# Two-layer encoder trunk on one core: a fifth opening block per feed-forward network, head stacks made in one step, and part of the mixer's weight splitting moved to GpSimd

## The chip, the cores and the metric

The kernel runs on one core of a Trainium2 chip. The metric is the device time of one execution in microseconds (us). The engines are named as the profile names them: PE is the matrix engine (PEld its weight loads), DVE the vector engine, ACT the scalar engine, POOL is GpSimd, and SP is the engine whose queue issues nearly all DMAs (copies between the chip's memory and the core's own).

## The reference

Two layers, each with three sub-layers on 512 tokens of width 1024. Every sub-layer stands between two RMS norms and is added to the running `x`.

```python
def reference(x, ...):
    for layer in range(2):
        h = swiglu(rms_norm(x, g[0]), ffn_w_in[layer, 0], ffn_w_out[layer, 0])
        x = x + 0.5 * rms_norm(h, g[1])
        h = token_mixer(rms_norm(x, g[2]), mix_w_in[layer], ...)
        x = x + rms_norm(h, g[3])
        h = swiglu(rms_norm(x, g[4]), ffn_w_in[layer, 1], ffn_w_out[layer, 1])
        x = x + 0.5 * rms_norm(h, g[5])

def swiglu(h, w_in, w_out):            # w_in 1024 x 5632, w_out 2816 x 1024
    g, u = jnp.split(h @ w_in, 2, axis=-1)
    return (jax.nn.silu(g) * u) @ w_out
```

The mixer projects `h` once (1024 to 3600 columns), feeds 8 attention heads (a mixture of three dilated windows) and 4 heads of a matrix memory (mLSTM, with gates from 16 of the columns), and sends both through one output projection. All values are float32.

## The kernel before

**Precision.** PE multiplies a reduced 32-bit type (`F32R`). Each factor is therefore split into a high part (ACT casts it) and a low part (DVE subtracts the high part from the original), and each product is three matmuls: high by high, high by low, low by high. For weights this is `split_w` (L114 the cast, L115 the subtraction) and `halves_of` (L97 and L99); for activations it is `put` (L209 and L210). The weight tiles `raw`, `hi` and `lo` are rings of three.

**Four token tiles.** The 512 tokens are four tiles of 128. After a sub-layer `post` adds its result to `x` tile by tile, and `pre` norms a tile for the next sub-layer, transposes it on PE (`tr`, L191) and puts high and low parts into `xh` and `xl`. Both get their inverse root from `rsqrt_sum`, whose power (`rs_yo`, `rs_yi`, L136) is computed by POOL. The last sub-layer's second half (tiles 2 and 3) overlaps the next one's start, which works on tiles 0 and 1.

**Feed-forward network (FFN).** `ffn_in` has 22 blocks `f` of 128 gate columns `g` and 128 up columns `u`, 512 KB of weights each. The first `ne` of them run plainly: `block(f, left)` for tiles 0 and 1, all `ne` in turn, then `block(f, right)` for tiles 2 and 3, all `ne` in turn, with 48 matmuls of 256 columns each; both weights are loaded anew for the second round. Then `xx.finish()` (a cast `xh`, L228, and a subtraction `xl`, L229, of a sum of activations `xf`) and the other blocks by `seven(f)`, a scheme with seven products for a pair of halves: 84 matmuls (L255 to L257) instead of the plain 96. A `seven` needs sums of its weights (`ws`, L319 to L322), split in turn into high and low (L297, L299). Its order on PE, DVE and ACT is written by hand; everything else is ordered by the framework's scheduler.

**A slot shared by weights and activations.** The `u` weight of a `seven` is loaded into the tile `wu`:

```python
raw = chunk("wu", 17 + 2 * (f % 2)) if gu and not whole_f else raw_tile()
```

The slots 17 and 19 also hold the two parts of `xf`. Slot 17 is last read in `finish()`, behind the last plain block, which also writes part of what `finish()` follows; slot 19 is last read when tile 3 is put, ahead of the right blocks. The weights of the block `ne + 1` go to the ring instead. All these loads go out through SP's one queue, in order (L272).

**Mixer.** Four groups of natural projections (`proj_nat`, matmuls `nat`, L500 to L502) on tiles 0 and 1, then transposed projections (`mixer_proj_T`), then the four groups on tiles 2 and 3, with the gates made between them (`gates` on DVE, transposes `gnat`, L727, on PE). The heads follow, while the attention's projections run between them. `stack_pair` makes, for each pair of attention heads, stacks of keys (`kst`) and queries (high `qsh`, low `qsl`) from two transposes on PE each; the scores `sc` (L870, L871) read them, `sm` is the softmax, `pt` its transpose.

Of the kernel before, what the change touches and what calls it, by code (L numbers as in the profile page):

```python
# [10 lines left out]
F32 = mybir.dt.float32  # L11
# [4 lines left out]
ALU = mybir.AluOpType  # L16
# [4 lines left out]
NT = S // P  # L21
# [20 lines left out]
def trunk_kernel(ctx, tc, x, norm_gain, ffn_w_in, ffn_w_out, mix_w_in, conv_w, conv_b,  # L42
# [48 lines left out]
    def raw_tile():  # L91
        return wp.tile([P, 1056], F32, tag="raw", name="raw", bufs=3)

    def halves_of(src, n, after=None):
        hi = wp.tile([P, 1056], F32R, tag="hi", name="hi", bufs=3)
        lo = wp.tile([P, 1056], F32R, tag="lo", name="lo", bufs=3)
        A.copy(hi[:, :n], src)  # L97
        with tc.issue_after(after) if after else nullcontext():
            V.tensor_tensor(lo[:, :n], src, hi[:, :n].bitcast(F32), ALU.subtract)  # L99
        return [[w[:, q: q + 512].rearrange("p (k c) -> p k c", k=4) for w in (hi, lo)] for q in range(0, n, 512)]  # L100

    def split_w(load, n, k4, pieces=1):
        raw = raw_tile()
        hi = wp.tile([P, 1056], F32R, tag="hi", name="hi", bufs=3)
        lo = wp.tile([P, 1056], F32R, tag="lo", name="lo", bufs=3)
        m = n * k4

        def view(w):
            return w[:, :m].rearrange("p (k c) -> p k c", k=k4)
        step = k4 // pieces  # L110
        for k in range(0, k4, step):
            r, h, l = [view(w)[:, k: k + step] for w in (raw, hi, lo)]
            load(r, k)
            A.copy(h, r)  # L114
            V.tensor_tensor(l, r, h.bitcast(F32), ALU.subtract)  # L115
        return view(hi), view(lo)

    def mm3(ps, lh, ll, rh, rl, start, stop):
# [50 lines left out]
            c = slice(n * 512, (n + 1) * 512)  # L169
            V.scalar_tensor_tensor(xs[:, t, c], y[:, c], r, xs[:, t, c], ALU.mult, ALU.add)  # L170

    first_nt = []

    def pre(t, xn, xx, ps_of):
        ss = small("pre_ss", 2)
        opening = len(first_nt) < 2
        if opening:
            V.tensor_tensor_reduce(out=xn[:, 512:1024], in0=xs[:, t, 512:1024], in1=xs[:, t, 512:1024], op0=ALU.mult,
                                   op1=ALU.add, scale=1.0, scalar=0.0, accum_out=ss[:, 1:2])
        for n in range(1 if opening else 2):  # L180
            A.activation(junk, xs[:, t, n * 512: n * 512 + 512], AF.Square, accum_out=ss[:, n: n + 1])
        r = rsqrt_sum((ss[:, 0:1], ss[:, 1:2]), D, EPS, "i")
        for hf in range(2):
            c = slice(hf * 512, hf * 512 + 512)
            V.scalar_tensor_tensor(xn[:, c], xs[:, t, c], r, gpre[:, c], ALU.mult, ALU.mult)
            if opening and hf:
                first_nt.append(last_ins(mybir.EngineType.DVE))
            ps = ps_of("tr")
            for k in range(4):
                kk = hf * 4 + k  # L190
                PE.transpose(ps[:, k * P: (k + 1) * P], xn[:, kk * P: (kk + 1) * P], ident)  # L191
            xx.put(t, hf, ps.rearrange("p (k c) -> p k c", k=4))
# [68 lines left out]
    def ffn_in(layer, j, xx, late=None):  # L261
# [17 lines left out]
                hts[f] = hts[f][:, 0:512]  # L279
            return hts[f]  # L280

        def block(f, c, pieces=1, after=None):
            h = h_of(f) if hts[f] is None else hts[f]
            banks = []
            for gu in range(2):
                lo_k, hi_k = halves_of(load(f, gu, pieces, True)[:, :1024], 1024, after)
                ps = psA("gu")[:, c]
                for q, w2 in enumerate((lo_k, hi_k)):
                    product(ps, w2, [x[:, 4 * q: 4 * q + 4, c] for x in (xx.h, xx.l)], q == 0)
                banks.append(ps)  # L290
            sil = t2("sil", f % 2)[:, c]
            A.activation(sil, banks[0], AF.Silu)
            V.tensor_tensor(h[:, c], banks[1], sil, ALU.mult)
# [87 lines left out]
            V.tensor_tensor(h[:, left], a, sil0, ALU.mult)  # L381
            V.tensor_tensor(h[:, right], u1, g1, ALU.mult)

        ne = 4
        for f in range(ne):
            block(f, left, 2 if late and f == 0 else 1, first_nt[-1] if late and f == 0 else None)
            if late and f < 2:
                late[f]()
        for f in range(ne):
# [92 lines left out]
            V.scalar_tensor_tensor(qk[b % 4][:, b // 4, :], th[:, :512], 1.0, y[:, :512], ALU.add, ALU.mult)  # L482
        return qk

    def proj_nat(layer, xx, col, n, evac, tiles=range(NT), ps_of=None, per=1):
        xh, xl = xx.h, xx.l
        w = mix_w_in[layer].rearrange("(k p) c -> p k c", p=P)
        parts = []
        for q in range(2):
            def load(dst, _, q=q):  # L490
                nc.sync.dma_start(dst, w[:, q * 4: q * 4 + 4, col: col + n])
            parts.append(split_w(load, n, 4))
        for t0 in tiles[::per]:
            ps = (ps_of or psA)("nat")
            for u in range(per):
                tok = slice((t0 + u) * P, (t0 + u + 1) * P)
                d = ps[:, u * n: (u + 1) * n]
                for k in range(NK):
                    wh, wl = parts[k // 4]
                    PE.matmul(d, xh[:, k, tok], wh[:, k % 4], start=k == 0, stop=False)  # L500
                    PE.matmul(d, xh[:, k, tok], wl[:, k % 4], start=False, stop=False)  # L501
                    PE.matmul(d, xl[:, k, tok], wh[:, k % 4], start=False, stop=k == NK - 1)  # L502
                    if k == 3:
                        yield
                if u == per - 1:
                    evac(t0, ps)
                yield
# [22 lines left out]
    def mixer(layer, xx):  # L530
# [40 lines left out]
            return go  # L571
        groups = ((3336, 264, evac_mo(1)), (2560, 256, evac_mv(0)), (2816, 256, evac_mv(1)), (3072, 264, evac_mo(0)))
        for n, g in enumerate(groups):
            run(proj_nat(layer, xx, *g, tiles=(0, 1), per=1 + (n in (1, 2))))
        qk = mixer_proj_T(layer, cvt, xx)
        run(proj_nat(layer, xx, *groups[0], tiles=(2, 3)))
        gates = mixer_gates(gt)
        next(gates)
        for n, g in enumerate(groups[1:]):
            run(proj_nat(layer, xx, *g, tiles=(2, 3), per=1 + (n < 2)))  # L580
            if n == 1:
                with tc.issue_after(last_ins(mybir.EngineType.PE)):
                    gates = next(gates)

# [36 lines left out]
        def stack_pair(hp):  # L621
            base = (20, 4)[hp % 2]
            ks = pair("kst", base)
            stack(kn, hp, ks, None)
            yield
            qh = pair("qsh", base + 1)
            ql = one.tile([P, D], F32R, tag="nt", name="qsl", bufs=2).rearrange("p (a s) -> p a s", a=2)
            stack(qn, hp, qh, ql)
            stacks[hp] = (ks, qh, ql)
            yield  # L630

        def projections():
            psN = banks_of(3, 4)
# [19 lines left out]
        def opening():  # L653
            for n, _ in enumerate(heads()):
                if n == 58:
                    run(stack_pair(0))
                if n in (60, 64):
                    next(att)
                yield
# [176 lines left out]
    def stack(src, hp, dh, dl):  # L836
# [9 lines left out]
        else:  # L846
            for e, s, o in ((0, lo, hi), (1, hi, lo)):
                A.copy(dh[s, e], ps[s])
                A.copy(dh[o, e], ps[s])
                V.tensor_tensor(dl[s, e], ps[s], dh[s, e].bitcast(F32), ALU.subtract)  # L850
                A.copy(dl[o, e], dl[s, e].bitcast(F32))

    def attention(stack_pair, stacks, pts, av, mask, mm):
        sms = {}
# [53 lines left out]
        for n in range(32 + lead + 1):  # L908
            if n < 32:
                scores(n)  # L910
                if n in (2, 9, 16):
                    made = stack_pair(1 + n // 7)
                if n in (2, 4, 9, 11, 16, 18):
                    next(made)
            m = n - lead
            if 0 <= m < 32:
                transposes(m)
# [15 lines left out]
    xx = Combined()  # L933
# [77 lines left out]
```

## Time and profile before

| | |
|---|---|
| Runs | 2124.03, 2122.1 and 2122.14 us, median 2122.14 |
| Profiled execution | 2122.1 us, of which the profile's span is 2120.1 and 2.0 lie around it |
| Busy PE, DVE, ACT, POOL | 2041.7, 1544.4, 1154.5, 253.6 us (96, 73, 54, 12%) |
| PE weight loads | 1861.2 us (88%), beside the matmuls |
| DMA | 270.28 MB, mean 127 GB/s |

PE's share is a share of time in which a matmul was in work, at whatever clock it ran. A view of windows gives, for a stretch of time, each engine's busy time with its number of instructions, then the granted share of PE's full clock, the share of the DMA engines' time and their rate. A view of waits names, for an engine's line, what ended its idle time, with the sum, the number and the longest.

### The profile page before, as it was taken

What the parts mean: (1) busy time and instruction counts of PE and PEld (TensorE: products, weight loads), DVE (VectorE), ACT (ScalarE), POOL (GpSimd) and SP (SyncE); (2) the same over time, 40 slices, a digit from 0 to 9 for tenths busy, and PEclk for the clock granted to TensorE, in tenths of its full rate; (3) what the DMA queues carried; (4) which work ended last, traced back from release to release, by engine and by line L of the source; (5) the groups of instructions that cost most, each with busy time, mean ns of one, the idle gap of its engine ahead of it and who ended that gap; (6) DMA issues with size and microseconds to landing.
All of it is one profiled execution on the core that took longest, in us unless ns stands there. A gap on an engine that the chain in (4) does not pass through costs nothing. (4 is left out here: it accounts for less than half of the span.)

```text
span 2120.1 us, 35561 instructions
## 1 busy us (share of the span) xinstructions
PE 2041.7 (96%) x13870; PEld 1861.2 (88%) x13870; DVE 1544.4 (73%) x2634; ACT 1154.5 (54%) x2058; POOL 253.6 (12%) x330
## 2 busy tenths in 40 slices
PE   8899999999999989999998999999999999899998
PEld 7899988889977889998898999888899779899886
DVE  7688757685767878876687886667856677788665
ACT  5455555445665645555554555554456755455554
POOL 1000001233512100000010000003434220000000
PEclk9999999999999999999999999999999999999999
DMA  7433355541113633335663334564411235333364
GB/s 217 123 111 100 110 188 193 143 122 58 53 51 119 190 110 107 113 102 187 188 188 107 105 100 129 188 192 126 119 53 41 88 122 160 110 104 115 120 205 144
DMA packets 297566, 270.28 MB, mean 127 GB/s; under 512 B 8661, under 2 KB 267189, under 8 KB 297398
## 3 DMA queue, kind: packets, MB, share of 16 engines
q1 hardware_dynamic: 297398, 268.01, 41.8%
q8 instruction: 108, 1.77, 0.3%
q14 instruction: 60, 0.49, 0.1%
HBM read 265.88 MB, written 2.10 MB: 126 GB/s over the span
## 5 line engine op out<-in xcount | busy, mean ns | idle before, releaser
L115 DVE TENSOR_TENSOR lo<-raw,hi 128x1024 fp32r<-128x1024 f32 (+1 forms) x280 | 348.8, 1246 | 241.4 <-ACT hi L114 241.3
L114 ACT CAST hi<-raw 128x1024 fp32r<-128x1024 f32 (+1 forms) x280 | 294.5, 1053 | 311.0 <-PE o L419 225.6
L417 PE MATMUL o<-lo,hq 128*128 128x512 f32 x704 | 236.9, 394 | 0.8 <-DVE lo L115 0.8
L419 PE MATMUL o<-hi,hq 128*128 128x512 f32 x704 | 223.3, 394 | 0.0
L416 PE MATMUL o<-hi,hq 128*128 128x512 f32 x704 | 210.6, 395 | 2.5 <-ACT hq L453 2.5
L297 ACT CAST hi<-ws 128x1024 fp32r<-128x1024 f32 x144 | 151.2, 1052 | 70.9 <-ACT a L297 62.1
L255 PE MATMUL pa<-tq,hi 128*128 128x256 f32 x576 | 164.6, 286 | 22.3 <-ACT hi L297 22.3
L500 PE MATMUL nat<-hi,xh 128*128 128x256 f32 (+1 forms) x640 | 184.9, 291 | 0.0
L501 PE MATMUL nat<-lo,xh 128*128 128x256 f32 (+1 forms) x640 | 182.0, 285 | 2.9 <-DVE lo L115 2.9
L502 PE MATMUL nat<-hi,xl 128*128 128x256 f32 (+1 forms) x640 | 181.6, 285 | 0.0
L299 DVE TENSOR_TENSOR lo<-ws,hi 128x1024 fp32r<-128x1024 f32 x144 | 175.2, 1219 | 1.5 <-ACT hi L297 1.5
L257 PE MATMUL pa<-tq,lo 128*128 128x256 f32 x576 | 165.0, 286 | 1.9 <-DVE lo L299 1.9
L256 PE MATMUL pa<-tq,hi 128*128 128x256 f32 x576 | 164.8, 286 | 0.0
L255 PE MATMUL pc<-xh,hi 128*128 128x256 f32 x576 | 163.6, 284 | 0.0
L257 PE MATMUL pc<-xh,lo 128*128 128x256 f32 x576 | 163.4, 284 | 0.0
L256 PE MATMUL pc<-xl,hi 128*128 128x256 f32 x576 | 163.4, 284 | 0.0
L416 PEld LDWEIGHTS o<-hi,hq 128*128 128x128 f32 x704 | 131.9, 188 | 34.0 <-ACT hq L453 3.4
L417 PEld LDWEIGHTS o<-lo,hq 128*128 128x128 f32 x704 | 131.9, 188 | 31.5 <-DVE lo L115 1.1
L419 PEld LDWEIGHTS o<-hi,hq 128*128 128x128 f32 x704 | 132.3, 188 | 30.8
L256 PE MATMUL gu<-xl,hi 128*128 128x256 f32 x512 | 147.4, 289 | 6.6 <-DVE xl L210 6.6
L255 PE MATMUL gu<-xh,hi 128*128 128x256 f32 x512 | 146.8, 290 | 4.6 <-ACT xf L236 3.7
L257 PE MATMUL gu<-xh,lo 128*128 128x256 f32 x512 | 146.3, 288 | 0.0
(242 smaller groups left out, 5660.3 us busy)
## 6 DMA issues: line engine op xcount, KB each, us to landing
raw<-in_ffn_w_out_dram SPq DMA_DIRECT2D x176, 512.0 KB, 3.5
raw<-in_ffn_w_in_dram SPq DMA_DIRECT2D x138, 512.0 KB, 3.9
wu<-in_ffn_w_in_dram SPq DMA_DIRECT2D x68, 512.0 KB, 4.0
raw<-in_mix_w_in_dram SPq DMA_DIRECT2D x56, 512.0 KB, 3.8
raw<-in_mix_w_out_dram SPq DMA_DIRECT2D x32, 512.0 KB, 3.7
raw<-in_mix_w_in_dram SPq DMA_DIRECT2D x16, 528.0 KB, 3.7
gpost<-in_norm_gain_dram SPq DMA_DIRECT2D x6, 512.0 KB, 5.9
gpre<-in_norm_gain_dram SPq DMA_DIRECT2D x5, 512.0 KB, 4.7
```

The source lines that it names most:

```text
L114: A.copy(h, r)
L115: V.tensor_tensor(l, r, h.bitcast(F32), ALU.subtract)
L255: PE.matmul(ps, wh[:, k], xh[:, k], start=start and k == 0, stop=False, skip_group_check=True)
L256: PE.matmul(ps, wh[:, k], xl[:, k], start=False, stop=False, skip_group_check=True)
L257: PE.matmul(ps, wl[:, k], xh[:, k], start=False, stop=k == 3, skip_group_check=True)
L299: V.tensor_tensor(lo, src, fp(hi), ALU.subtract)
L416: PE.matmul(banks[t][n], a, wh[:, n], start=first, stop=False)
L417: PE.matmul(banks[t][n], a, wl[:, n], start=False, stop=False)
L419: PE.matmul(banks[t][n], b, wh[:, n], start=False, stop=end)
L500: PE.matmul(d, xh[:, k, tok], wh[:, k % 4], start=k == 0, stop=False)
L501: PE.matmul(d, xh[:, k, tok], wl[:, k % 4], start=False, stop=False)
L502: PE.matmul(d, xl[:, k, tok], wh[:, k % 4], start=False, stop=k == NK - 1)
```

## The change

1. `ne` is 5 instead of 4: in each of the four FFNs one more block is computed plainly on the left and on the right, and one `seven` less.
2. In the mixer's first four groups (tiles 0 and 1) POOL instead of DVE computes the low part of every group's second half-weight: four subtractions a mixer, eight in all.
3. The second step of the gates (`gates = next(gates)`, with the transposes) is called behind the third instead of the second of the groups on tiles 2 and 3.
4. `stack_pair` makes keys and queries in one step, called at the scores 3, 13 and 17 instead of in two steps at 2 and 4, 9 and 11, 16 and 18; the last copy of a query's low part on ACT becomes a subtraction on DVE from PE's result.
5. At the start of the program, the sums of squares of the first two tiles are all on ACT, where DVE had the second half of each; and the first block's two low parts on DVE are no longer held behind the second tile's norm.

Line numbers from there on are lower by 1 to 10 in the changed kernel (L255 to L257 become L246 to L248, L272 becomes L263, L191 becomes L182, L839 becomes L828, L870 becomes L859, L115 becomes L114).

```diff
-    def halves_of(src, n, after=None):
+    def halves_of(src, n):
...
-        with tc.issue_after(after) if after else nullcontext():
-            V.tensor_tensor(lo[:, :n], src, hi[:, :n].bitcast(F32), ALU.subtract)
+        V.tensor_tensor(lo[:, :n], src, hi[:, :n].bitcast(F32), ALU.subtract)
...
-    def split_w(load, n, k4, pieces=1):
+    def split_w(load, n, k4, sub=None, pieces=1):
...
-            V.tensor_tensor(l, r, h.bitcast(F32), ALU.subtract)
+            (sub or V).tensor_tensor(l, r, h.bitcast(F32), ALU.subtract)
...
-        opening = len(first_nt) < 2
-        if opening:
-            V.tensor_tensor_reduce(out=xn[:, 512:1024], in0=xs[:, t, 512:1024], in1=xs[:, t, 512:1024], op0=ALU.mult,
-                                   op1=ALU.add, scale=1.0, scalar=0.0, accum_out=ss[:, 1:2])
-        for n in range(1 if opening else 2):
+        for n in range(2):
             A.activation(junk, xs[:, t, n * 512: n * 512 + 512], AF.Square, accum_out=ss[:, n: n + 1])
...
-            if opening and hf:
-                first_nt.append(last_ins(mybir.EngineType.DVE))
...
-        ne = 4
+        ne = 5
         for f in range(ne):
-            block(f, left, 2 if late and f == 0 else 1, first_nt[-1] if late and f == 0 else None)
+            block(f, left, 2 if late and f == 0 else 1)
...
-            parts.append(split_w(load, n, 4))
+            parts.append(split_w(load, n, 4, sub if q else None))
...
-            run(proj_nat(layer, xx, *g, tiles=(0, 1), per=1 + (n in (1, 2))))
+            run(proj_nat(layer, xx, *g, tiles=(0, 1), sub=G, per=1 + (n in (1, 2))))
...
-            if n == 1:
+            if n == 2:
                 with tc.issue_after(last_ins(mybir.EngineType.PE)):
                     gates = next(gates)
...
             stack(kn, hp, ks, None)
-            yield
...
             stacks[hp] = (ks, qh, ql)
-            yield
...
                 if n == 58:
-                    run(stack_pair(0))
+                    stack_pair(0)
...
-                A.copy(dl[o, e], dl[s, e].bitcast(F32))
+                V.tensor_tensor(dl[o, e], ps[s], dh[s, e].bitcast(F32), ALU.subtract)
...
-                if n in (2, 9, 16):
-                    made = stack_pair(1 + n // 7)
-                if n in (2, 4, 9, 11, 16, 18):
-                    next(made)
+                if n in (3, 13, 17):
+                    stack_pair((3, 13, 17).index(n) + 1)
```

**What the order of instructions says.** The rows below are instructions in the order in which an engine has them: line, operation, output and inputs with the program's numbers, and the shape.

First, SP's queue in the first FFN, before, from the third right block's `g` (`raw_652`) on; `raw_748` is the last load of a right block. `wu_786` is the `u` of block 4, the first `seven` (its `g` is `raw_784`), `wu_939` and `wu_1064` are those of the blocks 6 and 7:

```order
L272 DMA raw_652<-in_ffn_w_in_dram 128x8x128
L272 DMA wu_1064<-in_ffn_w_in_dram 128x8x128
L272 DMA raw_683<-in_ffn_w_in_dram 128x8x128
L272 DMA raw_717<-in_ffn_w_in_dram 128x8x128
L272 DMA raw_748<-in_ffn_w_in_dram 128x8x128
L272 DMA raw_784<-in_ffn_w_in_dram 128x8x128
L272 DMA raw_811<-in_ffn_w_in_dram 128x8x128
L272 DMA raw_813<-in_ffn_w_in_dram 128x8x128
L272 DMA wu_786<-in_ffn_w_in_dram 128x8x128
L272 DMA wu_939<-in_ffn_w_in_dram 128x8x128
```

After, from the second right block's `g` (`raw_653`) on; `raw_879` is the last load of a right block. `wu_917` is the `u` of block 5, now the first `seven` (its `g` is `raw_915`), in slot 19, and `wu_1069` that of block 7; block 6's are `raw_942` and, one row behind the last one here, `raw_944`:

```order
L263 DMA raw_653<-in_ffn_w_in_dram 128x8x128
L263 DMA wu_917<-in_ffn_w_in_dram 128x8x128
L263 DMA raw_684<-in_ffn_w_in_dram 128x8x128
L263 DMA raw_718<-in_ffn_w_in_dram 128x8x128
L263 DMA raw_749<-in_ffn_w_in_dram 128x8x128
L263 DMA raw_783<-in_ffn_w_in_dram 128x8x128
L263 DMA raw_814<-in_ffn_w_in_dram 128x8x128
L263 DMA raw_848<-in_ffn_w_in_dram 128x8x128
L263 DMA raw_879<-in_ffn_w_in_dram 128x8x128
L263 DMA raw_915<-in_ffn_w_in_dram 128x8x128
L263 DMA raw_942<-in_ffn_w_in_dram 128x8x128
L263 DMA wu_1069<-in_ffn_w_in_dram 128x8x128
```

The load of the first `seven`'s `u` has moved from behind all of the right blocks' loads to ahead of the last seven of them; the other three FFNs show the same.

Second, PE at the opening of the second FFN, before: the end of the fourth left block (`gu_7881`), the transposes of tile 3, and the first right block (`gu_7915`):

```order
L257 MATMUL gu_7881<-xh_7275,lo_7878 128x256
L191 MATMUL tr_7617<-idj_73,nt_7587 128x128 x4
L191 MATMUL tr_7628<-idj_73,nt_7587 128x128 x4
L255 MATMUL gu_7915<-xh_7275,hi_7911 128x256
L255 MATMUL gu_7946<-xh_7275,hi_7942 128x256
```

After, where `gu_7921` and `gu_7952` are the fifth left block:

```order
L248 MATMUL gu_7921<-xh_7280,lo_7918 128x256
L182 MATMUL tr_7622<-idj_73,nt_7592 128x128 x4
L246 MATMUL gu_7921<-xh_7280,hi_7917 128x256
L247 MATMUL gu_7921<-xl_7281,hi_7917 128x256
L182 MATMUL tr_7633<-idj_73,nt_7592 128x128 x4
L248 MATMUL gu_7921<-xh_7280,lo_7918 128x256
L246 MATMUL gu_7921<-xh_7280,hi_7917 128x256
L247 MATMUL gu_7921<-xl_7281,hi_7917 128x256
L248 MATMUL gu_7921<-xh_7280,lo_7918 128x256
L246 MATMUL gu_7952<-xh_7280,hi_7948 128x256
```

The transposes now stand inside the fifth left block, 18 matmuls later, and another 30 of that block's 48 matmuls stand between them and the first right block. The fourth FFN reads the same; in the third, the transposes stand 48 matmuls later, right ahead of the first right block as before.

Third, POOL at the start of the first mixer, before (`misc` and `smo` belong to the mixer's gate on its output; `rs_yo` and `rs_yi` are the inverse roots of tiles 2 and 3):

```order
L547 TENSOR_SCALAR misc_4175<-misc_4175 128x512
L136 TENSOR_TENSOR rs_yo_4082<-rs_uo_4080,mhalf_80 128x1
L560 TENSOR_TENSOR smo_4179<-smo_4179,misc_4175 128x248
L136 TENSOR_TENSOR rs_yi_4096<-rs_ui_4094,mhalf_80 128x1
L561 TENSOR_TENSOR smo_4179<-smo_4179,misc_4175 128x248
```

After:

```order
L538 TENSOR_SCALAR misc_4180<-misc_4180 128x512
L114 TENSOR_TENSOR lo_4199<-raw_4197,hi_4198 128x1056
L135 TENSOR_TENSOR rs_yo_4087<-rs_uo_4085,mhalf_80 128x1
L114 TENSOR_TENSOR lo_4269<-raw_4267,hi_4268 128x1024
L551 TENSOR_TENSOR smo_4184<-smo_4184,misc_4180 128x248
L135 TENSOR_TENSOR rs_yi_4101<-rs_ui_4099,mhalf_80 128x1
```

Two low parts stand ahead of tile 2's second inverse root, one of them ahead of its first; the other two stand around those of tile 3.

Two more places in words. On PE, the gates' transposes `gnat` stand behind the matmuls of the third group in both kernels, with the same rows around them. The transposes of the last stack (head pair 3) had the scores `sc` that read them right behind; in the changed kernel six matmuls of the output projection (`o`) and two `pt` stand between.

More of the change, by code (lines that the diff above doesn't have):

```diff
@@ L170, in post @@
             V.scalar_tensor_tensor(xs[:, t, c], y[:, c], r, xs[:, t, c], ALU.mult, ALU.add)
-    first_nt = []
     def pre(t, xn, xx, ps_of):
         ss = small("pre_ss", 2)
-        opening = len(first_nt) < 2
-        if opening:
-            V.tensor_tensor_reduce(out=xn[:, 512:1024], in0=xs[:, t, 512:1024], in1=xs[:, t, 512:1024], op0=ALU.mult,
-                                   op1=ALU.add, scale=1.0, scalar=0.0, accum_out=ss[:, 1:2])
-        for n in range(1 if opening else 2):
+        for n in range(2):
             A.activation(junk, xs[:, t, n * 512: n * 512 + 512], AF.Square, accum_out=ss[:, n: n + 1])
@@ L280, in h_of, with block @@
             return hts[f]
-        def block(f, c, pieces=1, after=None):
+        def block(f, c, pieces=1):
             h = h_of(f) if hts[f] is None else hts[f]
@@ L285, in block @@
             for gu in range(2):
-                lo_k, hi_k = halves_of(load(f, gu, pieces, True)[:, :1024], 1024, after)
+                lo_k, hi_k = halves_of(load(f, gu, pieces, True)[:, :1024], 1024)
                 ps = psA("gu")[:, c]
@@ L483, in mixer_proj_T, with proj_nat @@
         return qk
-    def proj_nat(layer, xx, col, n, evac, tiles=range(NT), ps_of=None, per=1):
+    def proj_nat(layer, xx, col, n, evac, tiles=range(NT), ps_of=None, sub=None, per=1):
         xh, xl = xx.h, xx.l
```

## The prediction

> **What bounds the kernel now.** I read the page first, then PE's waits, then windows around the places where PE waits, then the chain there.
>
> ```profile
> PE 2041.7 (96%) x13870; PEld 1861.2 (88%) x13870; DVE 1544.4 (73%) x2634; ACT 1154.5 (54%) x2058; POOL 253.6 (12%) x330
> ```
>
> PE is busy 96% of the span, so a change can gain only by fewer matmuls or in the idle 78 us and what follows them. PE's waits say where these are:
>
> ```profile
> PE pa L255 <- ACT hi L297: 22.3, 4, 5.7
> PE tr L191 <- DVE nt L185: 12.4, 6, 4.3
> PE gu L256 <- DVE xl L210: 6.6, 2, 3.6
> PE gnat L727 <- DVE gates L721: 5.3, 4, 1.6
> PE sc L870 <- ACT qsh L849: 3.9, 4, 1.3
> PE gu L255 <- ACT xf L236: 3.7, 1, 3.7
> PE nat L501 <- DVE lo L115: 2.9, 4, 1.1
> ```
>
> The columns are total, times, longest. `pa` is the first product of the first `seven`: each FFN waits once, 5.6 us. `tr` and `gu` <- `xl` are tiles 2 and 3 arriving late in the FFNs 2 to 4 and in the mixers.
>
> A wait also costs clock. In the windows (length; busy and instructions of PE, PEld, DVE, ACT, POOL; PE's clock; DMA share; GB/s) the first row is the first FFN's undisturbed part, then come its passage to the sevens, and the opening and the passage of the FFNs 2, 3 and 4:
>
> ```profile
> 90.00:120.00 30.00, 30.00 (x256) 30.00 (x255) 25.28 (x41) 16.51 (x29) 0.00 (x0) 1.00 0.37 106
> 60.00:90.00 30.00, 24.10 (x184) 23.59 (x183) 19.23 (x27) 12.28 (x20) 0.00 (x0) 0.89 0.42 123
> 720.00:750.00 30.00, 26.15 (x202) 25.37 (x202) 20.11 (x28) 13.69 (x20) 1.04 (x1) 0.94 0.56 164
> 750.00:780.00 30.00, 23.83 (x181) 23.33 (x180) 23.21 (x35) 13.36 (x21) 0.00 (x0) 0.89 0.37 108
> 1080.00:1110.00 30.00, 26.06 (x205) 25.36 (x204) 24.51 (x36) 15.69 (x24) 1.83 (x2) 0.94 0.60 177
> 1110.00:1140.00 30.00, 23.88 (x185) 23.38 (x184) 19.59 (x30) 12.53 (x19) 0.00 (x0) 0.89 0.38 110
> 1770.00:1800.00 30.00, 26.27 (x196) 25.83 (x197) 18.94 (x26) 12.82 (x19) 0.00 (x0) 0.89 0.50 141
> 1800.00:1830.00 30.00, 24.02 (x178) 23.52 (x177) 22.85 (x33) 13.35 (x21) 0.00 (x0) 0.83 0.37 106
> ```
>
> An undisturbed 30 us holds 256 matmuls, 0.117 us each. The four passages hold 184, 181, 185 and 178, so 72 + 75 + 71 + 78 = 296 too few: 34.7 us. The three openings hold 202, 205 and 196, 165 too few: 19.3 us; by idle time plus clock (30 − 26.15 + 0.06 × 30, and so on) they come to 5.7 + 5.7 + 7.0 = 18.4. Counting sees the time at half clock behind a wait, which the waits' list does not.
>
> What ends the wait at a passage is shown by the chain, here the fourth FFN's (start, us, what):
>
> ```profile
> 1798.89 1.06 ACT xh L228
> 1799.97 1.23 DVE xl L229
> 1801.22 3.75 DMA wu<-in_ffn_w_in_dram
> 1804.99 0.69 DVE ws L320
> ...
> 1807.52 1.05 ACT hi L297
> 1808.60 1.24 DVE lo L299
> 1809.88 0.58 PE pa L257
> ```
>
> The last plain matmul frees `finish()`, `finish()` frees slot 17, and only then is the first `seven`'s `u` loaded, summed and split. SP's queue in the first FFN says the same:
>
> ```profile
> 48.06 13.75 SPq L272 DMA_DIRECT2D raw<-in_ffn_w_in_dram  x6
> 68.64 5.97 SPq L272 DMA_DIRECT2D wu<-in_ffn_w_in_dram  x2
> ```
>
> The ring's loads were out by 62 us; `wu` is held to 68.64.
>
> **The change part by part**, against the profiled 2122.1 us (the median of the runs is 2122.14, so nothing needs to be shifted).
>
> *Passage to the sevens.* With block 5 first, `u` goes to slot 19, which is free once tile 3 is put, and SP has it ahead of the last seven right loads. So its landing (3.75 us), `ws`, and the splits run beside 3.5 right blocks of 48 × 0.117 = 5.6 us each. The wait on `wu` goes, and with it most of 34.7 us. Late next is `finish()`: 1.06 + 1.23 = 2.3 us, but its result is only read by the fourth product, 36 matmuls or 4.2 us in; and the last `hi` or `lo` of the ring, which can cost up to one 1.24 us per FFN. I take 0.5 per FFN, nearer to nothing because the weights are there, +2. The extra plain block is 96 matmuls for 84: 12 × 0.117 × 4 = +5.6. Sum −34.7 + 5.6 + 2 = −27, between −29 (no rest) and −20 (a rest of 2.3 us each, the whole of `finish()`). 1.05 MB more are loaded per FFN; a stretch of plain blocks alone bears that:
>
> ```profile
> 30.00:60.00 30.00, 30.00 (x257) 30.00 (x256) 24.21 (x33) 18.03 (x26) 0.00 (x0) 1.00 0.70 196
> ```
>
> PE is never idle there at 196 GB/s, the engines' DMA share is 0.70, DVE and ACT have 6 and 12 us to spare.
>
> *Openings of FFNs 2 to 4.* A fifth left block gives tile 3 another 48 × 0.117 = 5.6 us. Where the wait is on `xl` (2 times, at most 3.6), its 30 matmuls between transposes and right block are 3.5 us and the transposes themselves stand 2.1 later; where it is on `tr` (longest 4.3), they stand 5.6 later. Both cover. Of 18.4 to 19.3 I take −17, a rest of 2 where 3.5 meets 3.6 and clock follows; between −19 and −10 (half of it stays, if the chain of tile 3 is itself put back by the added block's splits on DVE).
>
> *POOL's low parts.* The mixers' starts wait for tile 3's transposes and for weights' low parts:
>
> ```profile
> 403.00:413.00 10.00, 6.96 (x38) 5.38 (x37) 6.73 (x8) 2.82 (x5) 3.96 (x4) 1.00 0.54 151
> 1452.00:1462.00 10.00, 7.50 (x36) 5.59 (x35) 7.01 (x8) 2.89 (x5) 3.95 (x4) 0.83 0.55 155
> 404.64 2.27 DVE L185 SCALAR_TENSOR_TENSOR nt<-xs,rs_yi,gpre 128x512 f32<-128x512 f32 x2
> 403.40 1.00 POOL L560 TENSOR_TENSOR smo<-smo,misc 128x264 f32<-128x264 f32 x1 [1.21 <-ACT smo L559]
> 11.37 1.42 DVE L185 SCALAR_TENSOR_TENSOR nt<-xs,rs_yi,gpre 128x512 f32<-128x512 f32 x2
> L810 POOL TENSOR_TENSOR hs<-hs,den 128x1024 f32<-128x1024 f32 x8 | 15.2, 1898 | 2.3 <-DVE den L808 1.9
> L115 DVE TENSOR_TENSOR lo<-raw,hi 128x1024 fp32r<-128x1024 f32 (+1 forms) x280 | 348.8, 1246 | 241.4 <-ACT hi L114 241.3
> ```
>
> The two starts lose 3.0 and 2.5 + 0.17 × 10 = 4.2: 7.2 us. DVE is relieved of eight subtractions of 1.25 = 10 us, and tile 3's transposes stand some 30 matmuls earlier with that work behind them. Against it: no row shows a POOL subtraction of this size; nearest is `hs`, 1.9 us, so each low part comes 0.65 later than on DVE at least, and `rs_yo` and `rs_yi` stand behind it. While POOL's `smo` ran, two `nt` on DVE took 2.27 in place of 1.42. I take −4, because relief and order both act on the wait that is there, between −7 (all of it goes) and +8 (below).
>
> [...]
>
> *Gates.* `gnat` stands behind the third group's matmuls on PE in both orders, so the wait on `gates` (5.3 us) stays: 0. No engine issues more for it.
>
> *Stacks.* At the last stack of each mixer PE waits on `qsh`:
>
> ```profile
> 623.00:631.00 8.00, 5.66 (x24) 3.84 (x24) 4.20 (x10) 5.84 (x13) 2.05 (x3) 0.78 0.23 69
> 1673.00:1681.00 8.00, 5.62 (x25) 3.94 (x23) 4.52 (x11) 6.31 (x14) 1.94 (x3) 0.86 0.23 66
> 1675.01 0.58 ACT qsh L848
> ```
>
> Idle plus clock are 2.34 + 0.22 × 8 = 4.1 and 2.38 + 0.14 × 8 = 3.5, together 7.6. Six `o` and a `pt` now stand between transposes and scores, over 2 us against waits of 1.3 at most; the second query stack still needs its 0.58 casts, 1 us per mixer. −5.5, between −7.6 and +2 (keys and queries in one step make PE wait at the two other stacks too, 0.5 each).
>
> [...]
>
> *Opening of the program.* Sums of squares move to ACT, and DVE's order becomes free:
>
> ```profile
> 4.95 0.69 DVE L178 CUSTOM_DVE_ANT_0 nt<-xs 128x512 f32<-128x512 f32 x1 [4.95 <-DMA xs<-in_x_dram]
> 12.70 2.35 DVE L99 TENSOR_TENSOR lo<-raw,hi 128x1024 fp32r<-128x1024 f32 x2
> ```
>
> DVE loses 2 × 0.69, but the two `lo` (2.35 us) now stand ahead of the second tile's `nt` (1.42, at 11.37), and the first product needs that tile. +1, in the lower half of 0 to +3 (2.35 and 0.69 in full), since the first tile's `nt` moves up by the 0.69 that DVE no longer spends on each tile, and the `lo` with it.
>
> Sum: −27 − 17 − 4 + 0 − 5.5 + 1 = −52.5; 2122.1 − 52.5 = 2069.6, given as 2069.
>
> **The rivals.**
>
> *POOL's low parts are the new wait.* In each mixer one stands ahead of tile 2's `rs_yo` and one ahead of its `rs_yi`, in POOL's queue, on the chain that PE already waits for: 2 × 1.9 = 3.8 us a mixer, 7.6 in both, in place of −4: 2069 + 11.6, some 2081. For it speaks the 2.27; against it that tile 3's chain, not tile 2's, ends the wait now. 0.17.
>
> *The passage gets a new wait.* In SP's queue `wu_1069` (block 7's `u`) stands ahead of `raw_944` (block 6's `u`) and needs slot 19, so it is held until block 5's `u` has been read by `ws`; if that is only at the passage, block 6's weights land 3.75 us late and PE waits inside the first `seven`, with clock 3.75 + 1.7 (0.11 × 30, halved because part falls in the wait). Four times 5.5 instead of 0.5: 2069 + 20 = 2089. It decides if `ws` comes after the last right block. Against it: `u` is there three blocks early. 0.13.
>
> *Slower than before.* The plain blocks become bound by loads. Each half block loads 1.05 MB in 5.6 us, which is 187 GB/s; there are now 10 in each FFN, 40 in all. Each would have to take 7.05 us, 149 GB/s, to eat 52.5 and another 4.2; at 145 they cost 7.24, 40 × 1.6 = 65 us, and the time is 2134. The row at 30 to 60 us (196 GB/s, share 0.70) speaks against it. 0.05, of which 0.02 end within 0.2%.
>
> *The gates do move.* If the second step's wait found cover after all, up to the 5.3 us and their clock go: 2062. 0.05.
>
> **How the numbers follow.** My forecast has 0.60, the rivals 0.17, 0.13, 0.05 and 0.05. 0.2% is 4.2 us, about what a measurement of this kernel can tell from no change. All cases but the third rival gain more: faster 0.95, same 0.02, slower 0.03. The range: all terms at their lower ends give 2122 − 29 − 19 − 7 − 7.6 = 2059, and 2056 with the gates partly covered; upward it takes in the first two rivals and a part of the bounds of openings and stacks with them, 2096.
>
> **What would show it.** Right: no wait of `pa` on `hi` above 1 us and 240 or more matmuls in the 30 us around each passage; `tr` and `gu` in the FFNs 2 to 4 waiting under 2 us in all; `gnat` still waiting 5 us; `sc` under 2.5. Wrong: `pa` or `pb` waiting for `hi` or `ws` at the passages (second rival), `rs_yo` or `rs_yi` waiting on POOL's `lo` in the mixers with `tr` or `nat` waiting longer (first), PE idle between left blocks with `raw` as the releaser (third). The prediction is most wrong if the sevens' first weights are ready early and yet the splits are ordered late.

## The result and the profile after

The changed kernel takes 2067.57 us (median of four runs, 2064.91 to 2072.16) against 2122.12 for the kernel before: a ratio of 0.9744, with a 95% interval of 0.9724 to 0.9764. The forecast was 2069. The profiled execution took 2064.91 us, of which the span is 2063.2; 57.2 us less than the profiled execution before.

The page's first part, after:

```profile
PE 2024.4 (98%) x13918; PEld 1848.6 (90%) x13918; DVE 1539.2 (75%) x2610; ACT 1140.9 (55%) x2034; POOL 269.3 (13%) x338
```

There are 48 matmuls more, as worked out, and PE is busy for 17.3 us less: fewer matmuls run at half clock (the mean granted clock is 0.995, before 0.982), and at half clock the same busy time held fewer of them: 18 in 3.41 us at 0.50 and 30 at 1.00, in two neighbouring stretches at a passage of the kernel before:

```profile
760.51:763.92 3.41, 3.41 (x18) 3.41 (x18) 3.38 (x5) 0.64 (x2) 0.00 (x0) 0.50 0.44 131
763.93:767.34 3.41, 3.41 (x30) 3.41 (x30) 1.34 (x3) 1.84 (x3) 0.00 (x0) 1.00 0.52 154
```

PE's waits after (total, times, longest):

```profile
PE tr L182 <- DVE nt L178: 9.1, 4, 4.8
PE gnat L716 <- DVE gates L710: 5.3, 4, 1.6
PE pt L875 <- ACT pts L880: 2.9, 4, 0.9
PE po L891 <- DVE qsl L840: 2.6, 2, 1.3
...
PE gu L247 <- DVE xl L201: 0.8, 1, 0.8
PE grev L721 <- ACT gn L719: 0.7, 2, 0.4
PE gu L246 <- ACT xh L200: 0.6, 1, 0.6
PE sc L859 <- ACT qsh L838: 0.5, 2, 0.2
```

The row `pa` <- `hi` (22.3 us) is gone. `tr` now stands for the program's opening (two of the four) and the mixers' starts alone; the FFNs wait for 0.8 + 0.6. `gnat` is as it was. `sc` <- `qsh` went from 3.9 to 0.5, but `po` <- `qsl`, 2.6 us, is new. `pt` <- `pts`, 2.9, is no loss against before: there `pt` waited about as long, for POOL:

```profile
PE pt L886 <- POOL sm L879: 2.7, 4, 0.9
```

Windows after, at the first FFN's passage, then opening and passage of the other three:

```profile
60.00:90.00 30.00, 30.00 (x255) 30.00 (x254) 21.29 (x28) 15.05 (x21) 0.00 (x0) 1.00 0.63 178
712.00:742.00 30.00, 30.00 (x256) 30.00 (x256) 24.16 (x32) 16.22 (x23) 2.00 (x1) 1.00 0.76 213
742.00:772.00 30.00, 30.00 (x256) 30.00 (x255) 26.02 (x39) 17.14 (x28) 0.00 (x0) 1.00 0.43 124
1067.00:1097.00 30.00, 28.61 (x240) 28.17 (x239) 22.22 (x28) 16.07 (x23) 1.06 (x1) 1.00 0.73 209
1097.00:1127.00 30.00, 30.00 (x256) 30.00 (x255) 25.88 (x40) 17.19 (x28) 0.00 (x0) 1.00 0.41 118
1732.00:1762.00 30.00, 30.00 (x255) 30.00 (x255) 24.25 (x33) 15.92 (x23) 0.00 (x0) 1.00 0.78 218
1762.00:1792.00 30.00, 30.00 (x255) 30.00 (x254) 25.97 (x40) 17.13 (x28) 0.00 (x0) 1.00 0.40 116
```

Every passage holds 255 or 256 matmuls, as the undisturbed stretch did. Only the third FFN's opening still misses 16. SP's queue in the first FFN shows why:

```profile
44.25 0.40 SPq L263 DMA_DIRECT2D wu<-in_ffn_w_in_dram  x1
46.92 21.96 SPq L263 DMA_DIRECT2D raw<-in_ffn_w_in_dram  x9
```

The first `seven`'s `u` goes out at 44 us, ahead of nine ring loads; before, its load was held to 68.64.

The stages in both profiled executions, from the first matmul of one kind to the first of the next (the last row: from the last `grev` to the last `sc`), summed over FFNs and mixers:

| Stage | before | after | difference | forecast |
|---|---|---|---|---|
| start to the first `gu` | 17.8 | 17.3 | −0.6 | +1 |
| plain blocks, first `gu` to first `pa` | 211.0 | 237.7 | +26.6 | |
| sevens, first `pa` to first `o` | 734.0 | 659.2 | −74.8 | |
| both together | 945.0 | 896.8 | −48.2 | −44 |
| mixers, first `nat` to the gates' first `grev` | 215.7 | 210.3 | −5.4 | −4 |
| heads and attention, last `grev` to last `sc` | 341.8 | 338.8 | −3.0 | −5.5 |

Each FFN has 96 matmuls more in its plain blocks (2 × 48 × 0.117 = 11.2 us) and 84 fewer in its sevens (9.8). Without these the plain blocks take 26.6 − 44.9 = −18.3 and the sevens −74.8 + 39.3 = −35.5.

### The profile page after: what moved, and what is told of

It is laid out like the page before. It is cut to its first block, busy times and chain, and to the rows that moved or that the text cites. A ratio compares the mean times of both kernels' runs of the same rounds, so it can differ in the third digit from the quotient of the medians.

```text
span 2063.2 us, 35639 instructions
## 1 busy us (share of the span) xinstructions
PE 2024.4 (98%) x13918; PEld 1848.6 (90%) x13918; DVE 1539.2 (75%) x2610; ACT 1140.9 (55%) x2034; POOL 269.3 (13%) x338
## 4 chain that ended last, share of the span: by engine, by line
PE 91%; DVE 4%; ACT 2%; issue 2%; DMA 0%; POOL 0%; SPq 0%; DVEq 0%; POOLq 0%; ACTq 0%
PE o L407 9%; PE o L410 9%; PE o L408 9%; PE pa L247 6%; PE pa L248 6%; PE pa L246 6%; PE gu L247 4%; PE gu L246 4%; PE gu L248 4%; PE pc L248 3%; PE pc L247 3%; PE pc L246 3%; PE nat L491 3%; PE nat L492 2%; PE nat L493 2%; PE po L891 2%
## 5 line engine op out<-in xcount | busy, mean ns | idle before, releaser
L114 DVE TENSOR_TENSOR lo<-raw,hi 128x1024 fp32r<-128x1024 f32 (+1 forms) x272 | 338.9, 1247 | 229.0 <-ACT hi L113 228.3
L246 PE MATMUL gu<-xh,hi 128*128 128x256 f32 x640 | 180.1, 284 | 0.7 <-ACT xh L200 0.6
L247 PE MATMUL gu<-xl,hi 128*128 128x256 f32 x640 | 179.9, 283 | 0.8 <-DVE xl L201 0.8
L248 PE MATMUL gu<-xh,lo 128*128 128x256 f32 x640 | 178.9, 282 | 0.0
L290 DVE TENSOR_TENSOR lo<-ws,hi 128x1024 fp32r<-128x1024 f32 x136 | 165.9, 1220 | 2.6 <-ACT hi L288 2.6
L248 PE MATMUL pa<-tq,lo 128*128 128x256 f32 x544 | 153.1, 281 | 0.0
L248 PE MATMUL pc<-xh,lo 128*128 128x256 f32 x544 | 153.0, 281 | 0.0
L247 PE MATMUL pa<-tq,hi 128*128 128x256 f32 x544 | 153.0, 281 | 0.0
L246 PE MATMUL pc<-xh,hi 128*128 128x256 f32 x544 | 153.0, 281 | 0.0
L247 PE MATMUL pc<-xl,hi 128*128 128x256 f32 x544 | 152.9, 281 | 0.0
L246 PE MATMUL pa<-tq,hi 128*128 128x256 f32 x544 | 152.4, 280 | 0.0
```

Source lines behind the costliest of these rows:

```text
L114: (sub or V).tensor_tensor(l, r, h.bitcast(F32), ALU.subtract)
L246: PE.matmul(ps, wh[:, k], xh[:, k], start=start and k == 0, stop=False, skip_group_check=True)
L247: PE.matmul(ps, wh[:, k], xl[:, k], start=False, stop=False, skip_group_check=True)
L248: PE.matmul(ps, wl[:, k], xh[:, k], start=False, stop=k == 3, skip_group_check=True)
L290: V.tensor_tensor(lo, src, fp(hi), ALU.subtract)
```

## The experiments

Medians are in us. The kernel before ran beside each group at 2122.33 (the first four), 2122.78 (the next four) and 2122.45 (the last four).

**The fifth block alone (e1).** The kernel before with one edit:

```diff
-        ne = 4
+        ne = 5
```

> The kernel before with five plain blocks and nothing else of the change. Theory (the passages' wait on slot 17 and the openings' late tile 3 are both cured by the fifth block): PE's lost time of about 35 us at the passages and 20 at the openings of FFNs 2 to 4 goes but for 2, 48 more matmuls cost 5.6, so 2122 - 35 - 18 + 5.6 = 2075, between 2071 and 2080; the stacks' and gates' waits stay as before. Rival (the gain came from the other parts, or needs them): above 2095.

Measured: 2070.15 (2068.69 to 2074.54), ratio 0.976, interval 0.9742 to 0.9778. That is just below the theory's range, so by the medians the fifth block is nearly the whole change: 52 of 54.6 us. `sc` <- `qsh` (3.9) and `gnat` (5.3) wait as before.

**The slot alone (e2).** The kernel before, four plain blocks, with `wu`'s two slots exchanged:

```diff
-            raw = chunk("wu", 17 + 2 * (f % 2)) if gu and not whole_f else raw_tile()
+            raw = chunk("wu", 19 - 2 * (f % 2)) if gu and not whole_f else raw_tile()
```

> The kernel before, still four plain blocks, with the two slots of wu exchanged, so that the first seven's u (block 4) goes to slot 19 and is no longer behind finish(). Theory (the slot alone makes the passage's wait): the 35 us of the passages go but for 0 to 4, nothing is added, the openings of FFNs 2 to 4 keep their 20: 2087 to 2091. Rival (the time between tile 3's arrival and the passage, which the fifth block lengthens, is what counts): less than 20 us gained, above 2102.

Measured: 2086.29 (2084.98 to 2087.72), ratio 0.9833 (0.9818 to 0.9847), just below the theory's range and far from the rival's. 36 us go with not one instruction added. Two of its passages, as windows:

```profile
754.00:784.00 30.00, 30.00 (x256) 30.00 (x255) 25.05 (x39) 16.28 (x27) 0.00 (x0) 1.00 0.37 107
1783.00:1813.00 30.00, 30.00 (x256) 30.00 (x255) 25.17 (x40) 16.39 (x28) 0.00 (x0) 1.00 0.37 107
```

They are full, while the openings still wait:

```profile
PE tr L191 <- DVE nt L185: 13.0, 6, 5.4
PE gu L256 <- DVE xl L210: 7.1, 2, 3.6
```

What the fifth block adds is therefore the openings' cover. By the medians that is 2086.29 − 2070.15 = 16 us net of its own matmuls, but the traces show only 10.8 of it in the FFNs (908.5 us in e2, 897.7 in e1, first `gu` to first `o`). The mixers of both traces take the same time within 1 us. e1's profiled run, at 2074.54, lies 4.4 above its median; its granted clock was 0.994, against 0.998 in the runs of 2068.69 and 2069.24. So the other 5 us are not shown to be the fifth block's.

**Six blocks (e3).** The changed kernel with `ne = 6`:

```diff
-        ne = 5
+        ne = 6
```

> The changed kernel with six plain blocks. The first seven is block 6, whose u goes to slot 17 again. Theory (slot): the wait behind finish() comes back in every FFN, 8.8 us each with its clock, plus 5.6 for 48 more matmuls, minus up to 2 at the third FFN's opening: 2067.6 + 35 + 5.6 - 2 = 2106, between 2100 and 2110. Rival (more plain blocks cover the passage, whatever the slot): 2067.6 + 5.6 - 2 = 2071.

Measured: 2106.09 (2105.41 to 2106.98), where the slot theory had 2106. PE's waits have the old row again:

```profile
PE pa L246 <- ACT hi L288: 23.0, 4, 6.1
```

One more block of cover, and the wait is back, because block 6's `u` falls on slot 17. Together with e2 this shows that what counts at the passage is that five is odd, not that it is one more than four.

**Low parts back on DVE (e5).** The changed kernel without `sub=G`:

```diff
-            run(proj_nat(layer, xx, *g, tiles=(0, 1), sub=G, per=1 + (n in (1, 2))))
+            run(proj_nat(layer, xx, *g, tiles=(0, 1), per=1 + (n in (1, 2))))
```

> The changed kernel with all low parts back on DVE in the mixer's first groups. Theory (POOL's low parts relieve DVE at the mixers' starts): the waits of tile 3's transposes and of projT come back, 8.5 us lost in two starts instead of 2.9, so 5.6 slower than the changed kernel: about 2073, between 2071 and 2076. Rival (the order around the starts did it, POOL's share brings nothing or costs): 2064 to 2069, with the starts losing under 4 us.

Measured: 2072.09 (2068.7 to 2073.71), within the theory's range and 3.0 to 4.5 above the changed kernel's two medians (2067.57, and 2069.11 in e12); the runs overlap. The first mixer's start, without POOL's low parts and with them:

```profile
388.00:418.00 30.00, 27.93 (x148) 23.41 (x148) 18.23 (x23) 11.59 (x19) 8.04 (x9) 0.94 0.44 122
```

```profile
388.00:418.00 30.00, 28.77 (x160) 24.69 (x159) 21.82 (x27) 13.57 (x22) 11.51 (x13) 1.00 0.48 135
```

From the first `nat` to the first `grev`, e5's two mixers take 216.2 us, those of the changed kernel 210.3. The five other traces with these low parts on POOL and the gates where they are (e3, e6, e7, e11, e12) have 210.0 to 210.3, so the stage shows what the overlapping runs do not. Some 3.5 of the 5.9 us are clock, by an estimate from windows: both of e5's starts have 0.94 in windows of 30 us, both of the changed kernel's 1.00. The price of it can be seen in the changed kernel. First POOL's rows, then DVE's at the same time:

```profile
383.44 2.52 POOL L114 TENSOR_TENSOR lo<-raw,hi 128x1024 fp32r<-128x1024 f32 x1
390.41 2.46 POOL L114 TENSOR_TENSOR lo<-raw,hi 128x1056 fp32r<-128x1056 f32 x1 [0.31 <-ACT hi L113]
```

```profile
383.65 2.34 DVE L137 SCALAR_TENSOR_TENSOR rs_ao<-rs_yo,rs_vo 128x1 f32<-128x1 f32 x1
...
390.17 0.21 DVE L137 SCALAR_TENSOR_TENSOR rs_ai<-rs_yi,rs_vi 128x1 f32<-128x1 f32 x1
390.42 2.47 DVE L138 SCALAR_TENSOR_TENSOR rs_yi<-rs_ai,rs_yi 128x1 f32<-128x1 f32 x1
```

Two operations on one column, `rs_ao` (L137) and `rs_yi` (L138), took 2.34 and 2.47 us here, to the end of POOL's subtraction (2.35 and 2.47 in the second mixer); their 22 other executions each in this trace took 0.21 to 0.22 and 0.14 to 0.16 us. By the kernel both read two inputs from SBUF, the core's memory that POOL's subtraction reads too; that this makes the difference is the author's reading, no run changed it alone. Two `nt` of 512 columns, which read one input (`o`) from PSUM, the memory that PE writes, took 0.69 us each within another of POOL's subtractions, where the mean of all 48 is 0.685:

```profile
370.25 2.48 POOL L114 TENSOR_TENSOR lo<-raw,hi 128x1056 fp32r<-128x1056 f32 x1 [11.40 <-ACT hi L113]
371.18 1.41 DVE L165 TENSOR_TENSOR nt<-o,gpost 128x512 f32<-128x512 f32 x2 [2.51 <-ACT junk L162]
```

The gain comes although tile 3's chain is held up twice, by 2.1 and 2.3 us.

**Two-step stacks again (e6).** The changed kernel with the old calls, the low part's copy still on DVE:

```diff
+            yield
...
+            yield
...
-                    stack_pair(0)
+                    run(stack_pair(0))
...
-                if n in (3, 13, 17):
-                    stack_pair((3, 13, 17).index(n) + 1)
+                if n in (2, 9, 16):
+                    made = stack_pair(1 + n // 7)
+                if n in (2, 4, 9, 11, 16, 18):
+                    next(made)
```

> The changed kernel with keys' and queries' stacks in two steps at the old places (the copy of the low part stays on DVE). Theory of the prediction (one step takes 5.5 us of waits away): 2073. Rival (the waits on qsh were replaced by waits of pt on pts and of po on qsl, 3.3 us per mixer in place of 3.7, plus one of 1.0 that went): 2067 to 2070, with the old waits of sc on qsh back.

Measured: 2063.24 (2062.76 to 2064.22). Neither number was right: undoing the one step, with the copy still on DVE, makes the kernel faster (e7 below, as fast as the changed kernel and on e6's chip, has 2067.4).

**The copy back on ACT (e11), and the changed kernel again (e12).** One step, but:

```diff
-                V.tensor_tensor(dl[o, e], ps[s], dh[s, e].bitcast(F32), ALU.subtract)
+                A.copy(dl[o, e], dl[s, e].bitcast(F32))
```

> The changed kernel with the last copy of the queries' low part back on ACT; keys and queries still in one step. If the copy on DVE is the part of the stacks' change that gains, and the one step the part that costs: 2069 to 2073, po or sc waiting longer for qsl. If the copy makes no difference: 2065 to 2069.

> The changed kernel again, beside the others on one chip: 2065 to 2070. If e6's 2063.2 is below the whole interval of this run, undoing the one step gains; if it is inside, the two can't be told apart by time.

Measured: 2060.32 (2060.23 to 2061.14) for e11, 2069.11 (2067.89 to 2069.37) for e12, on one chip. So the opposite of what e11 was to show: the copy on DVE is the part that costs, 8.8 us. With it on ACT the one step gains, by the stage: 334.3 us from the last `grev` to the last `sc`, against 340.0 to 342.0 in the three traces with the old stacks (the kernel before, e1, e2). e6's 2063.24 lies below all of e12. The two last score stacks' surroundings say how. First DVE and PE in the changed kernel, then in e11:

```profile
620.46 0.69 DVE L840 TENSOR_TENSOR qsl<-stk,qsh 64x512 fp32r<-64x512 f32 x1
621.21 1.95 PE L891 MATMUL po<-pts,av 128*64 128x256 f32 x16 [1.28 <-DVE qsl L840]
```

```profile
617.48 0.69 DVE L839 TENSOR_TENSOR qsl<-stk,qsh 64x512 fp32r<-64x512 f32 x1
618.64 1.95 PE L891 MATMUL po<-pts,av 128*64 128x256 f32 x16
```

`po` does not read `qsl`. But `stack` puts head pair 3 into PSUM bank 7 (`bank((5, 2, 2, 7)[hp], "stk")`), and `po` takes the same bank (`ps_po = banks_of(7)`). The new subtraction reads the bank once more, as the last of four DVE operations; the old copy read `dl` in SBUF. So `po` waits for it, 1.28 us, with the output projection's matmuls behind. Windows of 16 us there: the changed kernel, e12, and e11:

```profile
608.00:624.00 16.00, 13.02 (x72) 9.15 (x71) 11.80 (x25) 9.05 (x19) 3.44 (x5) 1.00 0.31 100
```

```profile
610.00:626.00 16.00, 13.02 (x65) 8.67 (x63) 11.07 (x24) 8.36 (x18) 3.46 (x5) 0.91 0.32 96
```

```profile
607.00:623.00 16.00, 14.33 (x80) 10.74 (x80) 10.40 (x23) 11.80 (x24) 3.49 (x5) 1.00 0.30 98
```

From the last `grev` to the last `sc`, e11's mixers take 334.3 us, e12's 342.0, the changed kernel's first trace 338.8, the kernel before 341.8. The 7.7 between e11 and e12 hold most of the 8.8. PE is idle for 1.5 us less in e11 (4.8 against 6.3, in both traces of the changed kernel). The changed kernel's two traces, with the same waits, differ by clock, 3.2 us. In e12 a stretch of 3.41 us at half clock follows `po`'s wait in each mixer; the first trace has none there. The stretches of 3.41 us around the wait, e12 and then the changed kernel's first trace:

```profile
619.78:623.20 3.42, 1.90 (x10) 0.87 (x10) 2.85 (x6) 1.40 (x3) 0.01 (x1) 0.99 0.02 5
623.20:626.61 3.41, 3.41 (x17) 1.74 (x14) 0.00 (x0) 0.23 (x1) 0.68 (x1) 0.51 0.00 0
```

```profile
617.60:621.01 3.41, 2.05 (x8) 1.07 (x8) 2.55 (x5) 1.90 (x4) 0.00 (x0) 1.00 0.02 7
621.01:624.42 3.41, 3.21 (x22) 2.18 (x23) 0.73 (x3) 0.37 (x1) 0.69 (x1) 1.00 0.00 0
```

The remaining 3 us stand in PE's busy time. The order of PE's matmuls differs there too, and what these 3 us come from was not separated.

**The old opening (e7).** The changed kernel with half of the first sums of squares on DVE, and the first low parts held back:

```diff
+        opening = len(first_nt) < 2
+        if opening:
+            V.tensor_tensor_reduce(out=xn[:, 512:1024], ...)
+        for n in range(1 if opening else 2):
...
+        with tc.issue_after(after) if after else nullcontext():
```

> The changed kernel with the old opening of the program: DVE has half of the first two tiles' sums of squares, and the first low parts wait behind the second tile's norm. Theory of the prediction (the new opening costs 1 us): 2066.5, with the first 20 us losing 9.6. Rival (it gains, since PE's lost time there is 10.6 after and 12.3 before): 2069, with the first 30 us losing about 12.

Measured: 2067.4 (2065.96 to 2068.97), no difference to the changed kernel. The first `gu` starts at 17.6 us here, at 17.3 and 17.7 in the changed kernel's two traces.

**Gates' second step later (e4).** The changed kernel, with the step moved behind eight steps of the attention's projections:

```diff
-            if n == 2:
-                with tc.issue_after(last_ins(mybir.EngineType.PE)):
-                    gates = next(gates)
...
+        run(take(proj, 8))
+        with tc.issue_after(last_ins(mybir.EngineType.PE)):
+            gates = next(gates)
-        paced(opening(), 67, take(proj, 32), 32, 1)
+        paced(opening(), 67, take(proj, 24), 24, 1)
```

> The changed kernel with the gates' second step behind the first eight steps of the attention's projections, that is behind one group more of matmuls, and the heads' opening filled with 24 steps of projections instead of 32. Theory (gnat waits for gates because no PE work stands between): the wait of 3.6 us and its clock, 12.8 us lost in two mixers, goes: 2055 to 2059. Rival (the heads lack the eight steps as filling later, or DVE is as late behind the group's low parts): 2064 to 2072.

Measured: 2077.31 (2074.53 to 2079.28), slower than both expected. `gnat` <- `gates` went, and the heads and the attention lack the filling:

```profile
PE stk L828 <- DVE kst L834: 4.0, 2, 2.0
PE st L118 <- DVE wt L776: 3.2, 4, 0.9
PE gnat L716 <- ACT hi L113: 3.1, 2, 1.5
```

**Gates' first step earlier (e8).** The changed kernel, with the first group on tiles 2 and 3 ahead of the transposed projections:

```diff
-        qk = mixer_proj_T(layer, cvt, xx)
         run(proj_nat(layer, xx, *groups[0], tiles=(2, 3)))
         gates = mixer_gates(gt)
         next(gates)
+        qk = mixer_proj_T(layer, cvt, xx)
```

> The changed kernel with the first group on tiles 2 and 3 and the gates' first step ahead of the transposed projections instead of behind them. Theory (gnat waits because the gates' chain on DVE starts too late, not for want of filling): the chain runs beside the transposed projections, gnat's waits of 3.6 us per mixer and their clock (12.8 us in both) go: 2055 to 2059. Rival (the chain's DVE work now delays the convolution or tile 3's parts, and PE waits there instead): 2064 to 2072.

Measured: 2051.25 (2050.55 to 2052.26), ratio 0.9663 (0.965 to 0.9676). 16.3 below the changed kernel, more than the 12.8 counted at the gates. Between the profiled executions it is 14.4: 10.5 from the first `nat` to `grev`, and 3.5 behind it, where the changed kernel still runs at half clock after its gates, to 481.06 us in the first mixer, and e8 does not. The first mixer's gates, in the changed kernel and here:

```profile
471.00:478.00 7.00, 3.92 (x28) 3.05 (x26) 5.08 (x9) 1.86 (x10) 4.93 (x3) 0.73 0.37 101
```

```profile
467.00:474.00 7.00, 7.00 (x63) 6.62 (x63) 2.45 (x2) 4.62 (x18) 4.21 (x5) 1.00 0.65 186
```

DVE has 5.08 us of work in the first and 2.45 in the second: the gates' chain is done when `gnat` comes (it ends at 430.07 us, and `gnat` starts at 470.1). Where filling is scarce, as here, starting the late engine's chain earlier gains what moving the reader later (e4) gives back.

**Together (e9, e10).** e9 is e8 with e6's stacks; e10 adds to e9 four plain blocks in the first FFN alone, with the slot counted from the first `seven`:

```diff
+        ne = 4 if late else 5
...
-            raw = chunk("wu", 17 + 2 * (f % 2)) if gu and not whole_f else raw_tile()
+            raw = chunk("wu", 19 - 2 * ((f - ne) % 2)) if gu and not whole_f else raw_tile()
...
-        ne = 5
```

> The changed kernel with the gates' first step ahead of the transposed projections and with the two-step stacks at the old places (the low part's copy stays on DVE). If the two gains stand on their own (2067.6 to 2051.3 for the gates, 2067.6 to 2063.2 for the stacks): 2047, between 2045 and 2049. If the stacks' gain was only a shift that the gates' move also changed: 2050 to 2053.

> The kernel e9_both with four plain blocks in the first FFN alone, where tile 3 is there early, and wu's slots counted from the first seven, so that it still has slot 19. Slot theory: the first passage has no wait either, and 12 matmuls less give 1.4 us: 2045.5. Rival (the first FFN needs the fifth block's time for its loads at the program's start): 2047 to 2054, with pa waiting for hi at 70 us.

Measured: 2050.16 (2048.78 to 2050.6) and 2049.02 (2047.61 to 2050.41). By the medians e6's stacks are worth 1.1 here, not 4.3, and the four blocks another 1.1; in both steps the runs overlap, so neither is clear of noise. e10's first passage is full, without the wait of `pa` that its rival expected, though its time lies in that rival's range:

```profile
52.00:82.00 30.00, 30.00 (x256) 30.00 (x255) 23.66 (x33) 15.89 (x24) 0.00 (x0) 1.00 0.59 167
```

e10 has the lowest median of all that ran, ratio 0.9657 (0.9644 to 0.967). e8 with e11's copy on ACT was not tried.

## Why the prediction was right, and where its terms were not

*Passages, −27 forecast.* −35.5 + 5.6 = −29.9: right in mechanism, shown by e2 and e3 from both sides. The rest of 0.5 us per FFN that was allowed for `finish()` didn't appear. The second rival (block 6's `u` held in SP's queue) had no trace: no `pa` or `pb` waits.

*Openings, −17 forecast.* −18.3, of which the first FFN has −0.7. What stays is the third FFN's, 0.8 + 0.6 in the waits.

*Load-bound blocks, the rival on the other side.* The rival needed the loads to be held to 149 GB/s. The opening windows show 209 to 218, with PE at 30.00 in two of three and the third explained by its waits for tile 3: nothing came near.

*POOL's low parts, −4 forecast.* −5.4 by the stages, −3.0 to −4.5 by e5's medians. The sign was right, but the price was weighed too low. The prediction counted low parts that come 0.65 us later and two `nt` of 2.27 us in place of 1.42; in the changed kernel one-column operations on DVE took 2.34 and 2.47 us, to the end of POOL's 2.52 and 2.46. Rows of the kernel before point the same way. DVE worked on beside four POOL operations in a row, but the fourth of them, beside two low parts on DVE, took 3.66 us where the second, of the same form, took 1.09:

```profile
482.72 3.66 POOL L561 TENSOR_TENSOR smo<-smo,misc 128x264 f32<-128x264 f32 x1
483.04 1.21 DVE L115 TENSOR_TENSOR lo<-raw,hi 128x1024 fp32r<-128x1024 f32 x1
```

But DVE did not stand still beside every low part: the two `nt` from PSUM took their 0.69 us. POOL took 2.47 us for a low part (the mean of the eight), not the 1.9 of the nearest row. The first rival did not come about: the starts got shorter. How much of the 5.4 is relief of DVE and how much the new order of tile 3's transposes was not separated.

*Gates, 0 forecast.* 5.3 us of waits before and after. The moved call changes nothing at all: the changed kernel built with the call behind the second group has the same instructions in the same order on every engine, but for the numbers of its buffers.

*Stacks, −5.5 forecast.* This is the step that failed. −3.0 in one trace of the changed kernel, +0.2 in the other, and in the three other traces with these stacks and the gates in place (e3, e5, e7) −1.0, −1.8 and +1.1. The waits that it counted did go (`sc` <- `qsh` from 3.9 to 0.5), and with the copy on ACT (e11) the stage gains 7.5, near its lower bound of −7.6. What it passed over is the moved copy, which it gave no price at all: a subtraction that reads PSUM in place of a copy that reads SBUF holds bank 7, and `po` waits. Two waits of 1.3 us, and in e12 a stretch at half clock behind each, took most of the term away; some 3 us of the stage's busy time stay unexplained (e11 above).

*Opening, +1 forecast.* −0.6 in the trace, nothing by e7. Below what could be told.

That the sum came out within 2 us is in part luck, since the terms missed in both directions: 7 us more than forecast went at the FFNs, the mixers' starts and the opening together, 2.5 to 5.7 less at the stacks, and the median of the runs 2.7 above the profiled one. The signs that the prediction named for being right all came: no wait of `pa`, 255 or 256 matmuls at each passage, 1.4 us of waits in the FFNs 2 to 4, `gnat` at 5.3 and `sc` at 0.5. None of them looked at `po`.

## What to carry to other kernels

When a load waits at the end of a stage, look first at which buffer it lands in and who read that buffer last: exchanging two slots was worth 36 us here without one instruction added, and one block more in the wrong parity gave it all back. An operation that moves to another engine has to be priced by what it reads as well: here a PSUM bank was not free for `po` until its last reader, moved to DVE, was done. A wait for a long chain on another engine was better met here by starting the chain earlier than by moving the reader later, since filling was scarce.

## What was not expected of the hardware

One-column operations on DVE with two inputs in SBUF, 0.21 and 0.15 us elsewhere in the changed kernel's trace, took 2.34 and 2.47 us while POOL subtracted 1024 and 1056 columns in SBUF. Two operations with an input from PSUM took their 0.69 us beside another such subtraction.

The same waits cost a different time in two executions of one kernel: at the last stacks, PE was busy for 13.02 of 16 us in both, with a granted clock of 1.00 and 72 matmuls in one and of 0.91 and 65 in the other. The traces of the kernel before and of the changed kernel show how. The clock in them is 1.00 or 0.50 and nothing between. Half clock came in stretches of 3.41, 6.83 or 10.24 us (but for the one at each program's end), thirteen times before and three times after, and within each trace these start whole multiples of 3.41 us apart. Where this grid lay against the program differed between the two executions of the changed kernel, and with it how the wait of `po` was split among its stretches: at the last stacks of the first mixer, the stretches shown above start at 617.60 and 621.01 us in the first trace, at 619.78 and 623.20 us in e12.

In the first trace of the changed kernel, the least busy stretch at the last stacks had PE busy for 2.05 us in the first mixer and for 2.12 in the second, and the clock stayed full. In e12's first mixer it was 1.90, and the next stretch had half clock. That is likely why the changed kernel's runs spread from 2064.91 to 2072.16 while those of e11, where `po` does not wait, lie within 1 us. No limit can be read from this: at the gates, whose `gnat` matmuls have 8 columns, a stretch with 2.24 us busy, from 470.82 us, came before half clock, and at the program's start one with 1.91 us, from 13.44 us, came before full clock. What decides the clock of a stretch stays open.

Half clock did not need a long wait either: at the changed kernel's gates no wait is longer than 1.6 us, and the clock granted from 471 to 478 us was 0.73; from 623 to 631 us of the kernel before, none is longer than 1.3, and 0.78 was granted.
